# A transformer step on one core: modulation rows spaced between written matmuls, and norms' spreads nine matmuls behind their sums

## The chip, the cores and the metric

The kernel runs on one core of a Trainium2 chip. The metric is the device time of one execution in microseconds (us), the median of the runs. The engines are TensorE (PE, matmuls; PEld its weight loads), VectorE (DVE), ScalarE (ACT), GpSimd (POOL) and SyncE (SP, which issues the loads); each works through its instructions in its own order, and semaphores between engines hold an instruction back until its inputs are there.

## What is computed

One step of a two-layer trunk on 640 tokens (128 context, 512 latent) of width 1024, all in float32. Cut to what matters here:

```
def adaln(cond, w, b):                       # six vectors of 1024 for each layer and each cond
    mod = jax.nn.silu(cond) @ w + b          # w: (1024, 6144)
    return jnp.split(mod[:, None, :], 6, axis=-1)
def modulate(x, g, shift, scale):
    return rms_norm(x, g) * (1 + scale) + shift
def swiglu(h, w_in, w_out):
    gt, up = jnp.split(h @ w_in, 2, axis=-1)
    return (jax.nn.silu(gt) * up) @ w_out
...
for l in range(2):
    sh1, sc1, g1, sh2, sc2, g2 = adaln(c, w_mod[l], b_mod[l])      # and the same for c_ctx
    h = modulate(x, norm1_g[l], sh1, sc1)
    o = ab_mixer(h) if l == 0 else attn(h)   # conv module || bidirectional mLSTM; attention
    x = x + g1 * o
    x = x + g2 * swiglu(modulate(x, norm2_g[l], sh2, sc2), w_ffn_in[l], w_ffn_out[l])
```

`cond` is `c` for latent and `c_ctx` for context tokens, so the modulation is a product of two vectors with a 1024 x 6144 matrix in each layer.

## The kernel before

**Tiling.** The activations lie transposed: 8 blocks of 128 features by 640 tokens, the tokens in two halves `a` of `HF` = 320. Each float32 operand is split into a high and a low part (ScalarE copies the high one, L112 for weights and L483 for activations; L115 and L484 subtract it), and `mm3` (L192) makes a product of three matmuls: L195, L196, L197. A weight tile is loaded into one of two `raw` buffers and split into one of six W buffers.

**Order in the program.** The stages follow one another: `ab_layer` (projections, convolution, mLSTM heads), `out_proj`, FFN 0 (`ffn_in`, then `ffn_out_T`), `attn_layer`, `out_proj`, FFN 1 (`ffn_in`, `ffn_out_rows`). The kernel is written so; a scheduler with a timing model of its own then sets the order of each engine's instructions, and `behind(ins)` tells it that what is issued inside has to stand behind the instructions `ins`. `so_far(engine)` is the last instruction written for an engine. All weight loads (`raw<-...`, `mraw<-in_wmod`) go through SP's queue in one order.

**The modulation.** Work on it is a list of generators in the background. The stages call `tick(us, dt)`, which adds `us` of credit and moves `now`; the generators run while there is credit. One that yields a negative number is not called again until `now` has moved by so much. For the first layer, `mod_T` makes 512 columns of the modulation at a time on TensorE: two groups of four matmuls (`mod_rows`, L254, `p<-mraw,cs`), each of which needs four loads of 256 KB into the ring of six `mraw` buffers; then `rows_T` (L270) transposes the rows on VectorE into a `t` buffer, and `mod_cols` (L261, `p<-t,fsel`) picks the columns with four small matmuls, to which L264 adds the bias. For everything behind out_proj the same is done on VectorE (`mod_blocks`, L225 and L227).

**The norms.** `norm_T` gives `tile(k, a)`, which squares a block (L379) and adds the squares up (L382), and `finish(a)`: the sums over the partitions by TensorE (L409, `p<-one,t`), the root on ScalarE (L412), the reciprocal on VectorE (L413), the spread of it over all partitions by TensorE (L417, `p<-ident,col`), then for each pair of blocks the product (L389), scale and shift (L429 on VectorE, L431 on ScalarE) and the split into `H` (L483, L484). There are two halves; `finish(1)` is put into `pending` and called inside the next stage by `pend`. `L497` adds a projection's result to the residual; L1592 is the silu of an FFN and L1593 its product. At the end of the mLSTM, L1154 transposes a head's output and L1156 and L1157 gate it.

Of the kernel before, what the change touches and what calls it, by code (L numbers as in the profile page):

```python
# [46 lines left out]
class Kern:  # L47
    def __init__(self, tc, I, O):
        self.tc, self.nc, self.I, self.O = tc, tc.nc, I, O
        self.psp, self.hold, self.hold_w, self.in_order = None, (), (), False  # L50
        self.bg, self.credit, self.now, self.lo_pool, self.lo_n, self.pending = [], 0.0, 0.0, (2, 3, 4, 5, 6, 7), 0, []
# [140 lines left out]
    def mm3(self, out, w, x, first, last):  # L192

        t = self.nc.tensor
        t.matmul(out, w[0], x[0], start=first, stop=False)  # L195
        t.matmul(out, w[0], x[1], start=False, stop=False)  # L196
        t.matmul(out, w[1], x[0], start=False, stop=last)  # L197
# [68 lines left out]

    def rows_T(self, ps):

        tr = self.rows_tr = self.tt()[:, :512]
        self.nc.vector.transpose(tr, ps)  # L270
        v = tr.rearrange("p (a q n) -> p a q n", q=4, n=32)
        return lambda q: v[:, :, q, 0:2]

    def mod_T(self, l, which, half, out):

        nc = self.nc
        j = 2 * which + half
        if (l, which) < (0, 5):
            ps = self.p1()
            for g in range(2):  # L280
                yield -3
                self.mfill()
                ks = range(4 * g, 4 * g + 4)
                ws = [self.mready.pop(0) for _ in ks]
                assert [key for key, _ in ws] == [(l, j, k) for k in ks]

                with self.tc.manual_schedule(engines={mybir.EngineType.PE}):
                    for (_, _, k), w in reversed(ws):
                        self.mod_rows(ps, k, w)
                self.mfill()  # L290
                yield 0.1
            yield -4
            parts = self.rows_T(ps)
            yield 0.6
        else:
            box = []
            yield from self.mod_blocks(l, j, box)
            r = self.st()[:, :32]
            for c in range(2):
                tr = self.tt()[:, :512]  # L300
                nc.vector.transpose(tr, box[0][:, c])
                nc.vector.tensor_reduce(r[:, c * 16:(c + 1) * 16], tr.rearrange("p (b i) -> p b i", i=32),
                                        axis=AX.X, op=ALU.add)
            v = r.rearrange("p (c a q) -> p a c q", c=2, q=4)
            parts = lambda q: v[:, :, :, q]
        yield -3
        self.mod_cols(l, which, half, out, parts)
        yield 0.1
# [57 lines left out]
    def norm_T(self, xT, m, H, gi):  # L366
# [17 lines left out]
        def finish(a):  # L384
            sl = slice(a * HF, (a + 1) * HF)
            r = self.rstd_P([sums[a][:, :HF]])
            for i in range(4):
# [45 lines left out]
    def pend(self, n):  # L433

        for _ in range(min(n, len(self.pending))):
            self.pending.pop(0)()

# [4 lines left out]
    def proj_A(self, H, *jobs, bg=()):  # L442
# [3 lines left out]
        for a in range(2):  # L446
# [3 lines left out]
            def mm(i, j, ks):  # L450
                w = jobs[i][0][j]
                if ks[0] == 0:
                    if self.pairs and len(jobs[i][0]) == 2:
                        if j == 0:
                            q = self.p2()
                            outs[i, 0], outs[i, 1] = q[:, 0, :HF], q[:, 1, :HF]
                    else:
                        outs[i, j] = self.p1()[:, :HF]
                for k in ks:
                    self.mm3(outs[i, j], (w[0][:, k * P:(k + 1) * P], w[1][:, k * P:(k + 1) * P]),  # L460
                             (H[:, k, 0, sl], H[:, k, 1, sl]), k == 0, k == KD - 1)

            for i, (ws, evac) in enumerate(jobs):
# [36 lines left out]
    def out_proj(self, H, xT, gate, last, norm, parts=(KD - 2,)):  # L500

        tile, finish = norm
        ws = self.wtake(3)

# [13 lines left out]
        for k0, k1 in zip((0,) + parts, parts):  # L518
            for i, a, ps in first:
                mm(ps, i, a, k0, k1)  # L520
                self.tick(8 / len(parts))
                if k1 == KD - 2:
# [8 lines left out]
        for a in range(2):  # L531
            for i in range(len(first) // 2, KD):
                if a == 0 and i > 2:
                    ws += self.wtake(1)
                ps = self.p1()[:, :HF]
                mm(ps, i, a, 0, KD)
                self.add_T(xT, i, a, ps, gate)
                tile(i, a)
                self.tick(5)
                if a == 1:  # L540
                    self.wdone(1)
                    if i == 3 + 0:
                        self.flush()
                        finish(0)
        self.pending.append(lambda: finish(1))
# [613 lines left out]
    def ab_layer(self, H, mods):  # L1159
# [132 lines left out]
        next(hd[1])  # L1292
        self.tick(5)
        next(hd[2])
# [6 lines left out]
        self.wcap = 2  # L1301
        o_in()
        next(hd[2])
# [40 lines left out]
    def attn_layer(self, H, mods):  # L1344
# [38 lines left out]
        for t in range(NT):  # L1383
            ps = self.p1()
            self.proj_B(ps, H, t, ws, 0, 512, 2, 512, 0, 4)
            self.pend(1)
            self.proj_B(ps, H, t, ws, 0, 512, 2, 512, 4)
            if t == 0:
# [228 lines left out]
    def ffn_out_T(self, fs, gs, xT, gate, norm=None):  # L1617

        ws = self.wtake(len(fs))
        for a in range(2):  # L1620
            for k in range(KD):
                ps = self.p1()[:, :HF]
                ks = slice(k * P, (k + 1) * P)
                for i, (g, w) in enumerate(zip(gs, ws)):
                    self.mm3(ps, (w[0][:, ks], w[1][:, ks]),
                             (g[:, a * HF:(a + 1) * HF], g[:, TOK + a * HF:TOK + (a + 1) * HF]),
                             i == 0, i == len(fs) - 1)
                self.add_T(xT, k, a, ps, gate)
                if norm:
                    norm[0](k, a)  # L1630
                    if (k, a) == (1, 1):
                        norm[1](0)
        if norm:
# [245 lines left out]
```

## Time and profile before

| | |
|---|---|
| median of 3 runs | 1563.33 us (1562.85 to 1564.67) |
| profiled execution | 1561.09 us, its span 1559.3 us |
| mean granted TensorE clock | 0.988 |
| TensorE busy | 1517.9 us (97%) |
| VectorE, ScalarE, GpSimd busy | 911.3, 580.9, 540.6 us |
| read from memory | 157.53 MB, 105 GB/s over the span |

Times of the trace count from the span's start. A row of the timeline gives start, duration, engine, line, operation, output and inputs, partitions and elements, the count of merged instructions, and in brackets the idle time of the engine just before it and what ended it. A matmul's duration includes its way through the array: they overlap, and the distance between two starts is what one costs. A row of waits gives who waited for whom: us in total, how often, the longest. A row of windows gives start and end, length, then the busy time of PE, PEld, DVE, ACT and POOL with counts, the granted clock, the share of the DMA engines and GB/s. A row of SP's queue gives the issue of the first load and the time up to the last.

### The profile page before, as it was taken

The numbers are of one execution on the slowest core, as the hardware profiler recorded it, in microseconds if no ns is written. First come the engines' busy times: TensorE is split into PE (matmuls) and PEld (weight loads), VectorE is DVE, ScalarE is ACT, GpSimd is POOL, SyncE is SP. The second block draws the span as 40 slices with busy tenths as digits, with TensorE's granted clock in tenths as the row PEclk, the third lists the DMA queues.
The fourth block names the chain that finished last, engine by engine and source line by source line (L and its number), as shares of the span: only waits on it lengthen the run. The fifth ranks groups of instructions, "written<-read, shape, count | busy, mean of one in ns | idle before, by whom it ended". The sixth has DMA issues, their size and how long they took to land.

```text
span 1559.3 us, 24243 instructions
## 1 busy us (share of the span) xinstructions
PE 1517.9 (97%) x9722; PEld 1411.1 (90%) x9722; DVE 911.3 (58%) x1514; ACT 580.9 (37%) x1151; POOL 540.6 (35%) x366
## 2 busy tenths in 40 slices
PE   8999999799999999999999999999999999999998
PEld 7889888679999999999998877799998998999996
DVE  5799523448983785637668588835663423333335
ACT  5756557225312221212126438624431221312123
POOL 3387312122222221222132455422225523334341
PEclk9999999899999999999999999999999999999999
DMA  9322122622542343314243220032321221312211
GB/s 368 126 100 93 61 89 90 229 98 95 200 152 83 121 155 103 130 60 154 91 166 118 82 81 28 22 128 82 109 95 55 81 82 55 108 55 93 70 68 68
DMA packets 63850, 165.36 MB, mean 106 GB/s; under 512 B 6904, under 2 KB 14112, under 8 KB 63738
## 3 DMA queue, kind: packets, MB, share of 16 engines
q1 hardware_dynamic: 63194, 163.16, 30.4%
q8 instruction: 76, 1.25, 0.3%
q10 hardware_dynamic: 544, 0.66, 0.1%
q14 instruction: 36, 0.29, 0.1%
HBM read 157.53 MB, written 6.26 MB: 105 GB/s over the span
## 4 chain that ended last, share of the span: by engine, by line
PE 82%; DVE 9%; ACT 3%; DMA 3%; issue 2%; POOL 1%; SPq 0%; ACTq 0%; DVEq 0%; POOLq 0%
PE p L195 25%; PE p L197 24%; PE p L196 24%; DVE cy L863 3%; PE p L254 1%; DMA mraw<-in_wmod 1%; PE p L1489 1%; DMA h<-in_xT 1%; DVE acc L227 1%; POOL t L872 1%; DVE H L484 1%; PE p L1509 1%; DVE h L497 1%; DMA h<-in_wmod 0%; ACT w L112 0%
## 5 line engine op out<-in xcount | busy, mean ns | idle before, releaser
L195 PE MATMUL p<-H,w 128*128 128x320 f32 (+1 forms) x1968 | 609.3, 311 | 4.0 <-DVE modT L264 1.6
L197 PE MATMUL p<-H,w 128*128 128x320 f32 (+1 forms) x1968 | 609.2, 310 | 0.0
L196 PE MATMUL p<-H,w 128*128 128x320 f32 (+1 forms) x1968 | 607.4, 309 | 0.6 <-DVE H L484 0.6
L115 POOL TENSOR_TENSOR w<-raw,w 128x1024 fp32r<-128x1024 f32 x124 | 310.4, 2508 | 751.1 <-ACT w L112 723.7
L195 PEld LDWEIGHTS p<-H,w 128*128 128x128 f32 x1968 | 371.0, 189 | 9.5 <-issue 1.7
L196 PEld LDWEIGHTS p<-H,w 128*128 128x128 f32 x1968 | 371.2, 189 | 1.6 <-DVE H L484 0.9
L197 PEld LDWEIGHTS p<-H,w 128*128 128x128 f32 x1968 | 370.8, 188 | 1.3 <-issue 1.1
L112 ACT ACTIVATE w<-raw 128x1024 fp32r<-128x1024 f32 x180 | 189.0, 1057 | 385.9 <-PE p L197 274.5
L227 DVE SCALAR_TENSOR_TENSOR acc<-mraw,cs,acc 128x512 f32<-128x512 f32 x196 | 176.8, 947 | 0.0
L1593 DVE TENSOR_TENSOR t<-t,p 128x320 f32<-128x320 f32 x88 | 42.6, 484 | 180.4 <-ACT t L1592 178.4
L1592 ACT ACTIVATE t<-p 128x320 f32<-128x320 f32 x88 | 38.3, 436 | 229.5 <-PE p L197 229.4
L115 DVE TENSOR_TENSOR w<-raw,w 128x1024 fp32r<-128x1024 f32 x56 | 78.3, 1399 | 64.2 <-ACT w L112 64.1
L497 DVE SCALAR_TENSOR_TENSOR h<-p,modT,h 128x128 f32<-128x128 f32 (+2 forms) x189 | 74.9, 431 | 60.2 <-PE p L197 59.9
L195 PE MATMUL p<-h,w 128*128 128x320 f32 x352 | 109.1, 310 | 0.0
L196 PE MATMUL p<-h,w 128*128 128x320 f32 x352 | 108.5, 308 | 0.0
L197 PE MATMUL p<-h,w 128*128 128x320 f32 x352 | 108.5, 308 | 0.0
L484 DVE TENSOR_TENSOR h<-t,h 128x320 fp32r<-128x320 f32 x88 | 85.9, 977 | 32.4 <-ACT h L483 32.4
L490 DVE TENSOR_TENSOR t<-p,h 128x512 f32<-128x512 f32 (+1 forms) x61 | 41.4, 681 | 83.7 <-PE p L197 83.6
L195 PE MATMUL p<-w,h 128*128 128x512 f32 (+1 forms) x224 | 87.9, 392 | 0.0
L196 PE MATMUL p<-w,h 128*128 128x512 f32 (+1 forms) x224 | 87.8, 392 | 0.0
L491 POOL TENSOR_TENSOR h<-h,t 128x512 f32<-128x512 f32 x50 | 69.5, 1394 | 51.9 <-DVE t L490 51.8
L197 PE MATMUL p<-w,h 128*128 128x512 f32 (+1 forms) x224 | 87.4, 390 | 0.0
(332 smaller groups left out, 2156.5 us busy)
## 6 DMA issues: line engine op xcount, KB each, us to landing
raw<-in_wfi SPq DMA_DIRECT2D x88, 512.0 KB
mraw<-in_wmod SPq DMA_DIRECT2D x160, 256.0 KB
raw<-in_wfo SPq DMA_DIRECT2D x44, 512.0 KB
raw<-in_wab SPq DMA_DIRECT2D x16, 512.0 KB
raw<-in_wc SPq DMA_DIRECT2D x12, 512.0 KB
h<-in_xT SPq DMA_DIRECT2D x14, 320.0 KB
h<-in_wmod SPq DMA_DIRECT2D x8, 512.0 KB
raw<-in_woab SPq DMA_DIRECT2D x8, 512.0 KB
```

What stands on the lines that cost most here:

```text
L112: self.hi_last = self.nc.scalar.activation(hi, r, AF.Copy).ins,
L115: e.tensor_tensor(lo, r, hi.bitcast(F32), ALU.subtract)
L195: t.matmul(out, w[0], x[0], start=first, stop=False)
L196: t.matmul(out, w[0], x[1], start=False, stop=False)
L197: t.matmul(out, w[1], x[0], start=False, stop=last)
L227: nc.vector.scalar_tensor_tensor(acc[:, c], w, s, bias if k == 0 else acc[:, c], ALU.mult, ALU.add)
L484: j = self.nc.vector.tensor_tensor(lo, src, hi.bitcast(F32), ALU.subtract)
L490: nc.vector.tensor_tensor(tmp, ps, gate, ALU.mult)
L491: (e or nc.gpsimd).tensor_tensor(x, x, tmp, ALU.add)
L497: self.nc.vector.scalar_tensor_tensor(x, ps[:, b - a * HF:e - a * HF], gate[:, k, c:c + 1], x, ALU.mult, ALU.add)
L863: nc.vector.scalar_tensor_tensor(y, u[:, i:i + CONV_N], w(i), y, ALU.mult, ALU.add)
L1593: nc.vector.tensor_tensor(s[:, sl], s[:, sl], pu, ALU.mult)
```

## The change

Three things are edited.

1. **The groups' pace.** A generator now waits six units of `now` between a set's two groups and none ahead of the first; in out_proj each piece gives credit by its number of blocks, and two `tick` calls in `ab_layer` give other numbers. Each group is set `behind` the last matmul written so far (`tied`, up to out_proj).
2. **The transposed rows** go into the first of the group's own `mraw` buffers instead of a `t` buffer.
3. **The norms.** `finish` becomes a generator that stops between the root and the spread. `pend` starts it (sums and root); `pend_rest`, called by the following stage after its first nine matmuls (after blocks 4 and 5 in attention's first stage), issues the rest behind them, and `mm3` sets the next product's first matmul behind the spread (`then`).

```diff
@@ mm3
-        t.matmul(out, w[0], x[0], start=first, stop=False)
+        with self.behind(self.then):
+            t.matmul(out, w[0], x[0], start=first, stop=False)
@@ rows_T
-    def rows_T(self, ps):
+    def rows_T(self, ps, tr=None):
 
-        tr = self.rows_tr = self.tt()[:, :512]
+        tr = self.rows_tr = self.tt()[:, :512] if tr is None else tr
@@ mod_T
             for g in range(2):
-                yield -3
+                if g:
+                    yield -6
...
-                with self.tc.manual_schedule(engines={mybir.EngineType.PE}):
+                with self.behind(self.so_far(mybir.EngineType.PE) if self.tied else ()), \
+                        self.tc.manual_schedule(engines={mybir.EngineType.PE}):
...
-            parts = self.rows_T(ps)
+            parts = self.rows_T(ps, ws[0][1])
@@ finish
-            r = self.rstd_P([sums[a][:, :HF]])
+            root = self.rstd_steps([sums[a][:, :HF]])
+            next(root)
+            yield
+            r = next(root)
@@ pend
-            self.pending.pop(0)()
+            g = self.pending.pop(0)()
+            if g:
+                next(g)
+                self.begun.append(g)
+
+    def pend_rest(self):
+
+        while self.begun:
+            with self.behind(self.so_far(mybir.EngineType.PE)):
+                for _ in self.begun.pop(0):
+                    pass
+            self.then = self.so_far(mybir.EngineType.PE)
@@ proj_A, in its loop over k (ffn_out_T the same with i == 2)
+                    if k == 2:
+                        self.pend_rest()
@@ out_proj
+        self.tied = False
...
-                self.tick(8 / len(parts))
+                self.tick(8 if len(parts) == 1 else (k1 - k0) * 0.45)
...
-                mm(ps, i, a, 0, KD)
+                mm(ps, i, a, 0, 3)
+                self.pend_rest()
+                mm(ps, i, a, 3, KD)
...
                     if i == 3 + 0:
+                        self.pending.append(lambda: finish(0))
+                        self.pend(1)
                         self.flush()
-                        finish(0)
@@ ab_layer
-        self.tick(5)
+        self.tick(5, 2)
...
-        o_in()
+        o_in(6, 14)
@@ attn_layer
             self.pend(1)
-            self.proj_B(ps, H, t, ws, 0, 512, 2, 512, 4)
+            self.proj_B(ps, H, t, ws, 0, 512, 2, 512, 4, 6)
+            self.pend_rest()
+            self.proj_B(ps, H, t, ws, 0, 512, 2, 512, 6)
@@ ffn_out_T
-                        norm[1](0)
+                        self.pending.append(lambda: norm[1](0))
+                        self.pend(1)
```

The edits shift the lines: L195 to L197 become L196 to L198, L254 and L261 become L255 and L262, L382 becomes L385, L389 L395, L409 L415, L412 L418, L413 L419, L417 L423, L429 L435, L484 L503, L497 L516, L1593 L1618.

What the built programs show at four places follows. In the first, TensorE's order in out_proj of the first layer before (`mraw,cs` the groups, `t,fsel` the columns, `ident,h` the transposes of the mLSTM's output):

```order
L261 MATMUL p_3141<-t,fsel 32x8 x4
L254 MATMUL p_3147<-mraw,cs 32x512 x8
L261 MATMUL p_3210<-t,fsel 32x8 x4
L254 MATMUL p_3216<-mraw,cs 32x512 x4
L1154 MATMUL p_3266<-ident,h 128x128
L1154 MATMUL p_3265<-ident,h 128x128 x4
L254 MATMUL p_3216<-mraw,cs 32x512 x4
L1154 MATMUL p_3277<-ident,h 128x128
```

And around one of its groups now:

```order
L197 MATMUL p_3411<-H,w 128x320
L198 MATMUL p_3411<-H,w 128x320
L255 MATMUL p_3365<-mraw,cs 32x512 x4
L196 MATMUL p_3455<-H,w 128x320
L197 MATMUL p_3455<-H,w 128x320
L198 MATMUL p_3455<-H,w 128x320
```

A group that stood beside other groups now stands between written products of out_proj; the next group's or columns' matmuls are 45 or more matmuls away, and the whole layer's twelve groups are placed like this, eight of them ahead of out_proj.

The second is SP's queue of loads around out_proj, before (`woab` out_proj's weights, `wfi` those of FFN 0):

```order
L99 DMA raw<-in_woab 128x1024 x3
L99 DMA mraw<-in_wmod 128x512 x24
L1326 DMA out_new_n<-s 8x128
L99 DMA raw<-in_wfi 128x1024 x8
L99 DMA mraw<-in_wmod 128x512 x4
```

And now:

```order
L99 DMA raw<-in_woab 128x1024 x3
L99 DMA mraw<-in_wmod 128x512 x8
L1349 DMA out_new_n<-s 8x128
L99 DMA mraw<-in_wmod 128x512 x3
L99 DMA raw<-in_wfi 128x1024
L99 DMA mraw<-in_wmod 128x512 x2
L99 DMA raw<-in_wfi 128x1024 x2
L99 DMA mraw<-in_wmod 128x512 x4
```

The run of 24 loads of the modulation is now in pieces of two to eight, earlier in the program or between the loads of FFN 0's weights.

The third is VectorE at FFN 0's start, the second half of its norm, before:

```order
L382 TENSOR_TENSOR t<-t 128x320 x2
L497 SCALAR_TENSOR_TENSOR h<-p_3707,modT,h 128x320
L382 TENSOR_TENSOR t<-t 128x320
L413 RECIPROCAL col<-col 128x3
L389 TENSOR_TENSOR t<-h,p_3810 128x640 x4
L1593 TENSOR_TENSOR t<-t,p_3778 128x320
L429 TENSOR_SCALAR t<-t,modT 128x320 x4
L484 TENSOR_TENSOR h<-t,h 128x320
L484 TENSOR_TENSOR H<-t,H 128x2x320 x3
```

And now:

```order
L385 TENSOR_TENSOR t<-t 128x320 x2
L516 SCALAR_TENSOR_TENSOR h<-p_3701,modT,h 128x320
L385 TENSOR_TENSOR t<-t 128x320
L419 RECIPROCAL col<-col 128x3
L1618 TENSOR_TENSOR t<-t,p_3772 128x320
L503 TENSOR_TENSOR h<-t,h 128x320
L395 TENSOR_TENSOR t<-h,p_3818 128x640 x4
L435 TENSOR_SCALAR t<-t,modT 128x320 x4
L503 TENSOR_TENSOR H<-t,H 128x2x320 x2
```

The silu's product (L1618) and its split (L503, `h<-t,h`) now stand ahead of the norm's four products (L395) instead of behind them.

The fourth is TensorE at attention's start, before:

```order
L195 MATMUL p_8358<-w,H 128x512
L196 MATMUL p_8358<-w,H 128x512
L197 MATMUL p_8358<-w,H 128x512
L409 MATMUL p_8371<-one_87,t 128x1 x3
L417 MATMUL p_8378<-ident,col 128x128 x2
L417 MATMUL p_8378<-ident,col 128x64
L195 MATMUL p_8432<-w,H 128x512
```

And now:

```order
L196 MATMUL p_8352<-w,H 128x512
L197 MATMUL p_8352<-w,H 128x512
L198 MATMUL p_8352<-w,H 128x512
L415 MATMUL p_8365<-one_87,t 128x1 x3
L423 MATMUL p_8378<-ident,col 128x128 x2
L423 MATMUL p_8378<-ident,col 128x64
L196 MATMUL p_8352<-w,H 128x512
```

The sums and the spread still stand next to each other; both now come two blocks (six matmuls) ahead of the end of the first 24 matmuls, where they stood behind all 24.

More of the change, by code (lines that the diff above doesn't have):

```diff
@@ L49, in __init__ @@
         self.tc, self.nc, self.I, self.O = tc, tc.nc, I, O
-        self.psp, self.hold, self.hold_w, self.in_order = None, (), (), False
+        self.psp, self.hold, self.hold_w, self.in_order, self.begun, self.then, self.tied = None, (), (), False, [], (), True
         self.bg, self.credit, self.now, self.lo_pool, self.lo_n, self.pending = [], 0.0, 0.0, (2, 3, 4, 5, 6, 7), 0, []
@@ L1627, in ffn_out_T @@
                              i == 0, i == len(fs) - 1)
+                    if i == 2:
+                        self.pend_rest()
                 self.add_T(xT, k, a, ps, gate)
```

## The prediction

> **What bounds the kernel now.** I read the page first, for which engine carries the time, then the list of waits of TensorE, then the timeline around each wait, and last the stages' windows, for the clock.
>
> ```profile
> PE 1517.9 (97%) x9722; PEld 1411.1 (90%) x9722; DVE 911.3 (58%) x1514; ACT 580.9 (37%) x1151; POOL 540.6 (35%) x366
> PE 82%; DVE 9%; ACT 3%; DMA 3%; issue 2%; POOL 1%; SPq 0%; ACTq 0%; DVEq 0%; POOLq 0%
> ...
> PE p L254 <- DMA mraw<-in_wmod: 9.9, 5, 3.5
> PE p L417 <- DVE col L413: 5.3, 5, 2.3
> PE p L1067 <- ACT s L1109: 1.0, 1, 1.0
> PE p L905 <- DVE t L270: 0.8, 1, 0.8
> ```
>
> TensorE is busy for 1517.9 of the 1559.3 us, and the change removes no matmul. So only two things can be won: the idle time of TensorE (1559.3 − 1517.9 = 41.4 us, part of it at the ends) and time that it spends at half clock. The two largest single waits are those the change aims at: the rows of the modulation (L254) waiting for their loads, 9.9 us in 5 waits, and the spread of a norm's root (L417) waiting for the reciprocal, 5.3 us in 5. Most of the first lies in the output projection (out_proj) of the first layer, so I opened that stretch:
>
> ```profile
> 301.12 1.07 PE L254 MATMUL p<-mraw,cs 128*32 128x512 f32 x8 [1.47 <-DMA mraw<-in_wmod]
> 305.68 1.94 PE L254 MATMUL p<-mraw,cs 128*32 128x512 f32 x8 [3.50 <-DMA mraw<-in_wmod]
> 308.53 0.30 PE L261 MATMUL p<-t,fsel 128*32 128x8 f32 x8 [0.92 <-DVE t L270]
> 311.06 1.94 PE L254 MATMUL p<-mraw,cs 128*32 128x512 f32 x8 [2.24 <-DMA mraw<-in_wmod]
> 313.85 1.11 PE L1154 MATMUL p<-ident,h 128*128 128x128 f32 x4 [0.45 <-DVE h L1156]
> 316.40 1.94 PE L254 MATMUL p<-mraw,cs 128*32 128x512 f32 x8 [1.44 <-DMA mraw<-in_wmod]
> 322.67 0.41 PE L195 MATMUL p<-H,w 128*128 128x320 f32 x1 [0.74 <-DVE h L1157]
> ...
> 302.50:319.60 17.10, 8.89 (x42) 3.07 (x43) 3.76 (x7) 0.74 (x1) 0.00 (x0) 0.50 0.55 187
> 290.84 29.85 SPq L99 DMA_DIRECT2D mraw<-in_wmod  x24
> ```
>
> The number in brackets is the idle time before a row. Together they make 10.76 us. The queue row says why: 24 loads in one run, 29.85 / 24 = 1.24 us each, so a group of four needs 5.0 us, while its matmuls last 1.07. The window row adds the second cost: over 17.10 us the granted clock is 0.50, and a group takes 1.94 instead of 1.07 us.
>
> **The change, part by part.**
>
> **Groups apart, in out_proj.** Before, six groups stand nearly back to back there. After, the twelve groups of the whole layer are spread; four are left in out_proj, with 45 or more matmuls between neighbours. A matmul of 320 columns starts every 0.15 us (rows of 373.46 and 373.61, below), so 45 of them last 6.6 us, which is the smallest distance between two groups; four loads take 5.0. The loads' waits (8.65 us) and the wait for the rows' transpose (0.92) go. What stays is the end of the mLSTM: 0.45 and 0.74 are waits for its outputs, and its ten transposes now stand in one piece, with no group between them to cover VectorE; I add 0.8 and keep 2.0 us idle. That gives 10.76 − 2.0 = 8.8. The half clock: 8.89 us of work at 1.94/1.07 of its length is 8.89 × (1 − 1.07/1.94) = 4.0 too long; with 2.0 us of waits left I keep one half chance of a short period at half clock (0.9) and count 3.1. **Sum +11.9**; ends: 5 (loads at half the rate, below) and 14.
>
> **The other eight groups, in the layer's projections.** Their waits are in these rows:
>
> ```profile
> 240.70 1.06 PE L254 MATMUL p<-mraw,cs 128*32 128x512 f32 x8 [1.23 <-DMA mraw<-in_wmod]
> 150.00:290.00 140.00, 135.43 (x937) 121.29 (x939) 66.73 (x157) 83.61 (x226) 42.23 (x29) 0.96 0.31 99
> ```
>
> The 1.23 and the 0.8 before L905 go with the groups that caused them. Against that, ScalarE's order now mixes sigmoid and silu, two table loads more (1.28 each, row of 372.29 below); ScalarE is busy for 83.61 of 140 us, so I let a fifth of them reach TensorE. The loads now enter SP's queue earlier, and four of them stand between the first and the second weight tile of the V projection; four loads are 5.0 us, and the group that frees their buffers now stands 72 matmuls (10.6 us) ahead of that projection, so I cost it at nothing, covered by those matmuls; without that cover up to 5.0. The transposed rows now lie in one of the six load buffers until L261 has read them, so one buffer comes free later: five are enough for a group of four. **Sum +1.5**; ends −5.0 (all of the V tiles' delay) and +4 (also the 1.0 of L1067).
>
> **FFN 0: spread nine matmuls behind the sums.**
>
> ```profile
> 349.44 0.85 PE L417 MATMUL p<-ident,col 128*128 128x128 f32 x6 [1.04 <-DVE col L413]
> 371.25 0.72 PE L409 MATMUL p<-one,t 128*128 128x1 f32 x6
> 372.54 0.88 PE L417 MATMUL p<-ident,col 128*128 128x128 f32 x6 [0.56 <-DVE col L413]
> 373.46 0.31 PE L196 MATMUL p<-H,w 128*128 128x320 f32 x1
> 373.61 0.31 PE L197 MATMUL p<-H,w 128*128 128x320 f32 x1
> ...
> 372.29 1.28 ACT L1592 ACT_TABLE_LOAD   x1
> 373.58 0.44 ACT L1592 ACTIVATE t<-p 128x320 f32<-128x320 f32 x1
> 373.45 3.01 DVE L389 TENSOR_TENSOR t<-h,p 128x640 f32<-128x640 f32 x4 [0.97 <-PE p L417]
> 376.38 0.48 DVE L1593 TENSOR_TENSOR t<-t,p 128x320 f32<-128x320 f32 x1
> 378.21 0.48 DVE L484 TENSOR_TENSOR h<-t,h 128x320 fp32r<-128x320 f32 x1
> 378.61 2.29 DVE L484 TENSOR_TENSOR H<-t,H 128x640 fp32r<-128x640 f32 x3
> 481.21 0.39 PE L195 MATMUL p<-H,w 128*128 128x320 f32 x1 [1.59 <-DVE modT L264]
> ```
>
> Nine matmuls last 9 × 0.147 = 1.32 us, more than the 0.56 and the 1.04 that were waited: +1.60. But VectorE's order changes with it. Call T the end of the sums (371.97). Before, L389 begins at T + 1.5 and the first quarter of the second half of H is ready at T + 7.45 (378.61 + 0.8); 48 matmuls and the spread stand before its first reader, at T + 8.3, so 0.9 is to spare. After, the silu product (L1593) and its split (L484 h) stand ahead of L389. They wait for the root (0.3), the table load (1.28), silu (0.44), the product (0.48), the copy on ScalarE (about 0.45) and the split (0.48): L389 begins at T + 3.65, and H is ready 5.2 later (the same work less those two), at T + 8.8. The reader comes at T + 7.8. New wait 1.05, a little more for the later quarters: −1.15. TensorE then comes to the modulation's wait at 481.21 earlier than VectorE does: −0.7; and the sums may wait 0.2. **Sum −0.5**; ends −3.5 and +1.6.
>
> **Attention's start.**
>
> ```profile
> 826.49 0.85 PE L417 MATMUL p<-ident,col 128*128 128x128 f32 x6 [0.82 <-DVE col L413]
> 841.71 0.40 PE L197 MATMUL p<-w,H 128*128 128x512 f32 x1
> 841.95 0.39 PE L195 MATMUL p<-w,H 128*128 128x512 f32 x1
> 844.16 0.83 PE L409 MATMUL p<-one,t 128*128 128x1 f32 x6 [0.18 <-DVE t L382]
> 845.55 0.88 PE L417 MATMUL p<-ident,col 128*128 128x128 f32 x6 [0.56 <-DVE col L413]
> ...
> 827.38:844.10 16.72, 16.37 (x96) 14.61 (x95) 16.51 (x28) 10.39 (x22) 3.60 (x2) 1.00 0.38 139
> ```
>
> Here the change works against itself. The first spread loses its 0.82 us of waiting, but stands 1.32 behind the sums, 0.5 later than before, and it starts a chain on VectorE that has no gap: 16.51 of 16.72 us busy until the squares are summed. So the second half's sums can begin at 844.16 + 0.5 = 844.66. TensorE would reach them at 841.95 − 0.82 = 841.13, because they now stand six matmuls of 0.23 us earlier; and the spread follows them at once, as before. It waits 3.5, then 0.56, and then has the six matmuls to do (1.4): it stands at 848.14 where it stood at 846.24, **−1.9**. A wait of 3.5 us should also halve the clock, for which the nearest row is this one:
>
> ```profile
> 1063.89 1.51 PE L417 MATMUL p<-ident,col 128*128 128x128 f32 x6 [2.30 <-DVE col L413]
> 1063.90:1067.10 3.20, 3.20 (x13) 3.20 (x14) 1.66 (x3) 0.80 (x2) 0.48 (x1) 0.50 0.65 230
> 1063.59 0.16 DVE L413 RECIPROCAL col<-col 128x3 f32<-128x3 f32 x1
> 1098.49 0.42 PE L196 MATMUL p<-H,w 128*128 128x320 f32 x1 [0.62 <-DVE H L484]
> ```
>
> Idle for 2.30 us was enough there for 3.20 us at clock 0.50, which is 1.6 us of work lost; I take **−1.6** at attention's start. Ends for both: −5 and +0.8.
>
> **FFN 1.** The 2.30 shrinks by the nine matmuls to 2.30 − 1.32 = 0.98, since the reciprocal is itself late (1063.59, 2.0 after the sums): +1.3. With 0.98 idle the 3.20 us at half clock should go (+1.6), as none followed the 1.04 at 349.44. The second spread now stands nine instead of 23 matmuls behind its sums, so H comes earlier and the 0.62 goes. **Sum +3.5**; ends +1 and +4.
>
> [...]
>
> **Together** 11.9 + 1.5 − 0.5 − 1.9 − 1.6 + 3.5 = 12.9 us. The profiled execution took 1561.09 us (span 1559.3 and 1.8 around it) and would take 1548.2. It stands 2.2 below the median of the runs, 1563.33; from the median the sum gives 1550.4.
>
> **The rivals.**
>
> *The clock stays low.* Waits of 2.0 us in out_proj and 0.98 in FFN 1 are shorter than 2.30, but the window 150:290 shows a mean clock of 0.96 with no TensorE wait above 1.23 in it, so 2.30 is no threshold. If both places keep a period at half clock, 0.9 + 0.7 in out_proj's remainder and 1.6 in FFN 1 are lost: gain 9.7, 1553.6. Chance 15%.
>
> *The loads are still late.* They now share the queues with weight tiles, as they did not in the run of 24. At twice the time for each, 2.5 us, a group needs 10 where the shortest distances are 6.6 and 8.7: some 4.7 us of waits and half of the 4.0 at low clock remain, gain about 6.2, 1557.1. Against it: the 24 loads moved 6 MB in 29.85 us, a rate the mixed queue has no reason to halve. Chance 10%. If the layer's loads come as late as before, the change does not do what it says: only the norms' parts remain, −0.5 of them net, and the time is within 0.2% of 1563 (that bound, 3.1 us, is about what a measurement of this kernel can tell from no change). Chance 7%.
>
> *More is won.* The low clock in 150:290 is worth 2 × 0.04 × 140 = 11 us at half speed, 5.6 us of work. If evenly placed groups keep TensorE fed there, half to all of it comes back: 1545 to 1548. Nothing shows that the groups caused it. Chance 13%.
>
> *Slower.* Each transposed group must have been through VectorE (L270) before L261 stands on TensorE, now written straight ahead of the next group. If VectorE, which works through its orders in sequence, is late, all of TensorE's work stands behind L261. The rows show 0.8 and 0.92 for two of these waits. Six of them must last 12.9 / 6 = 2.2 us each to eat the gain, and 2.7 to be measured as slower; at 3 us the time is 1568. Against it: 40 to 70 matmuls, 6 us or more, lie between a group's last rows and its L261, and VectorE is busy for 67 of 140 us. Chance 6%.
>
> **How the numbers follow.** The forecast has the other 49%, its own range is 1547 to 1553.5, and its time, 1550.4, is the prediction. The range 1542 to 1559 leaves out the last two cases with no gain and the far ends of the others, some 18%. Faster: 49 + 15 + 10 + 13 = 87, less 2 for loads worse than doubled: 85%. Same 8%, slower 7%.
>
> **What would show it.** Right: no wait of L254 for its loads above 0.5 us and clock 1.00 in out_proj; the spread's waits gone at FFN 0, but 1 us before the first matmul on the second half of H; sums at attention's start waiting 3 to 4 us, with a period at 0.50 behind; at FFN 1 a wait near 1 and clock 1.00. Wrong: waits of L261 for VectorE, of TensorE for V's weight tiles near 60 to 75 us, or a junction wait at FFN 0 of 3 us.

## Result: 1545.6 us, 1.1% faster

| | before | changed |
|---|---|---|
| median, runs made together | 1563.77 us (4 runs) | 1545.63 us (4 runs, 1544.78 to 1550.6) |
| ratio to before | | 0.9891, 95% interval 0.9869 to 0.9912 |
| profiled execution | 1561.09 us | 1544.78 us |
| span | 1559.3 us | 1542.8 us |
| TensorE busy | 1517.9 us | 1511.4 us |
| mean granted clock | 0.988 | 0.994 |

The profiled executions differ by 16.3 us, the medians by 18.1; the sum of the prediction, 12.9, is held against the first. These are the page's first row and the head of TensorE's waits after the change:

```profile
PE 1511.4 (98%) x9722; PEld 1407.5 (91%) x9722; DVE 912.9 (59%) x1514; ACT 581.6 (38%) x1153; POOL 540.9 (35%) x366
...
PE p L415 <- DVE t L385: 3.6, 1, 3.6
PE p L196 <- ACT t L861: 1.9, 2, 1.7
PE p L679 <- POOL ident masks.py:199: 1.6, 1, 1.6
PE p L415 <- DVE t L654: 1.6, 1, 1.6
PE p L196 <- DVE modT L265: 1.6, 1, 1.6
PE p L423 <- DVE col L419: 1.3, 2, 0.8
PE p L197 <- POOL w L115: 1.3, 1, 1.3
```

The busy time alone fell by 6.5 us although every matmul is still there: that is time at half clock that is gone (a mean granted clock of 0.994 instead of 0.988). The other 10 us of the span are idle time. The loads of the groups, 9.9 us before, have left the head of the list; a wait for the sums of a norm (L415) now leads it.

**Where it came from.** The matmuls of `mm3` are numbered from 0 in order of time in both traces, and the starts of the n-th are compared. The cuts at 1400, 4600 and 5500 lie shortly ahead of the first sums of a norm, so that each norm falls into one row. The table gives by how much the changed kernel is ahead, and what each stretch adds:

| up to | n | before, us | changed, us | ahead by | stretch |
|---|---|---|---|---|---|
| within the V projection | 300 | 82.57 | 87.82 | -5.3 | -5.3 |
| rest of the first layer, with out_proj's first matmuls | 1200 | 292.62 | 292.11 | +0.5 | +5.8 |
| most of out_proj, to FFN 0's first sums | 1400 | 345.33 | 329.06 | +16.3 | +15.8 |
| FFN 0 and its norm, to attention's first sums | 4600 | 823.56 | 805.87 | +17.7 | +1.4 |
| attention and its norm, to FFN 1's first sums | 5500 | 1057.96 | 1045.20 | +12.8 | -4.9 |
| FFN 1's norm and its first matmuls | 6100 | 1158.61 | 1142.12 | +16.5 | +3.7 |

Two of the groups (2 x 1.06 us) moved from behind the 1200th matmul to ahead of it, so out_proj itself won 13.7 and the layer 2.6. In out_proj the rows that answer to the seven waits of before are these, and the window's clock:

```profile
296.94 1.06 PE L255 MATMUL p<-mraw,cs 128*32 128x512 f32 x8 [0.87 <-DMA mraw<-in_wmod]
301.05 0.66 PE L1177 MATMUL p<-ident,h 128*128 128x128 f32 x4 [0.51 <-DVE h L1180]
310.30 1.07 PE L255 MATMUL p<-mraw,cs 128*32 128x512 f32 x8
319.39 1.06 PE L255 MATMUL p<-mraw,cs 128*32 128x512 f32 x8
...
290.00:340.00 50.00, 48.61 (x345) 44.07 (x342) 27.11 (x59) 18.70 (x42) 14.15 (x9) 1.00 0.42 143
150.00:290.00 140.00, 137.99 (x1000) 122.77 (x998) 69.59 (x159) 88.05 (x234) 43.64 (x30) 1.00 0.36 119
```

Of 10.76 us of waits 1.38 are left, the clock is 1.00 where it was 0.50 for 17.1 us, and a group takes 1.06 instead of 1.94. The last row is the layer ahead of it: its clock went from 0.96 to 1.00, which the forecast had left to a rival.

Where the change lost, the profile of before had shown it at one place and not at the other. Attention's start:

```profile
827.27 0.83 PE L415 MATMUL p<-one,t 128*128 128x1 f32 x6 [3.58 <-DVE t L385]
828.66 1.54 PE L423 MATMUL p<-ident,col 128*128 128x128 f32 x6 [0.56 <-DVE col L419]
...
828.10:834.90 6.80, 6.24 (x19) 5.17 (x19) 4.73 (x11) 2.91 (x11) 0.00 (x0) 0.50 0.13 45
```

The sums wait 3.58 us, the spread 0.56, and 6.80 us at clock 0.50 follow. And the V projection, here TensorE's rows and SP's queue:

```profile
53.19 0.39 PE L196 MATMUL p<-H,w 128*128 128x322 f32 x1 [1.05 <-ACT h L437]
59.72 0.42 PE L196 MATMUL p<-H,w 128*128 128x322 f32 x1 [1.71 <-ACT t L861]
78.92 0.50 PE L197 MATMUL p<-w,H 128*128 128x512 f32 x1 [1.27 <-POOL w L115]
...
48.02 0.33 SPq L99 DMA_DIRECT2D raw<-in_wv  x1
58.02 1.75 SPq L99 DMA_DIRECT2D mraw<-in_wmod  x4
59.82 11.99 SPq L99 DMA_DIRECT2D raw<-in_wv  x3
...
60.10:63.50 3.40, 3.40 (x15) 3.40 (x14) 3.07 (x6) 1.98 (x6) 0.00 (x0) 0.50 0.90 273
```

Four loads of the modulation are sent only at 58.02, when the group at 56.94 has read their buffers, and three of the four weight tiles of V stand behind them in the same queue; the split (L115) of one of them is then late at 78.92. But the weight tiles are the smaller part. At the 200th matmul, ahead of V, 4.9 us are already lost: the two waits for ScalarE (1.05 and 1.71, where before had 0.42), 1.7 of the 3.4 us at half clock, and the group's own 1.06, which before came behind that point.

### The profile page after: what moved, and what is told of

Same layout as the page of the kernel before. It is cut to its first block, busy times and chain, and to the rows that moved or that the text cites. A ratio compares the mean times of both kernels' runs of the same rounds, so it can differ in the third digit from the quotient of the medians.

```text
span 1542.8 us, 24258 instructions
## 1 busy us (share of the span) xinstructions
PE 1511.4 (98%) x9722; PEld 1407.5 (91%) x9722; DVE 912.9 (59%) x1514; ACT 581.6 (38%) x1153; POOL 540.9 (35%) x366
## 4 chain that ended last, share of the span: by engine, by line
PE 83%; DVE 6%; ACT 4%; DMA 3%; POOL 2%; issue 2%; SPq 0%; ACTq 0%; DVEq 0%; POOLq 0%
PE p L196 25%; PE p L198 25%; PE p L197 25%; POOL t L895 2%; PE p L255 1%; DMA raw<-in_wab 1%; ACT w L112 1%; PE p L1514 1%; DVE cy L886 1%; POOL w L115 1%; PE p L1534 1%; DVE H L503 1%; DMA h<-in_wmod 0%; PE p L1536 0%; PE p L1535 0%
## 5 line engine op out<-in xcount | busy, mean ns | idle before, releaser
L196 PE MATMUL p<-H,w 128*128 128x320 f32 (+1 forms) x1968 | 609.5, 311 | 5.1 <-ACT t L861 1.9
L198 PE MATMUL p<-H,w 128*128 128x320 f32 (+1 forms) x1968 | 608.8, 310 | 0.0
L197 PE MATMUL p<-H,w 128*128 128x320 f32 (+1 forms) x1968 | 606.9, 309 | 0.0
L115 POOL TENSOR_TENSOR w<-raw,w 128x1024 fp32r<-128x1024 f32 x124 | 312.0, 2521 | 738.6 <-ACT w L112 723.1
L196 PEld LDWEIGHTS p<-H,w 128*128 128x128 f32 x1968 | 370.0, 188 | 15.2 <-issue 3.4
L198 PEld LDWEIGHTS p<-H,w 128*128 128x128 f32 x1968 | 370.1, 188 | 1.3 <-issue 1.1
L197 PEld LDWEIGHTS p<-H,w 128*128 128x128 f32 x1968 | 370.5, 188 | 0.7 <-issue 0.2
L1618 DVE TENSOR_TENSOR t<-t,p 128x320 f32<-128x320 f32 x88 | 42.5, 483 | 181.1 <-ACT t L1617 180.7
L115 DVE TENSOR_TENSOR w<-raw,w 128x1024 fp32r<-128x1024 f32 x56 | 79.3, 1416 | 67.4 <-ACT w L112 67.3
L196 PE MATMUL p<-h,w 128*128 128x320 f32 x352 | 109.1, 310 | 0.0
L197 PE MATMUL p<-h,w 128*128 128x320 f32 x352 | 108.5, 308 | 0.0
L198 PE MATMUL p<-h,w 128*128 128x320 f32 x352 | 108.5, 308 | 0.0
L516 DVE SCALAR_TENSOR_TENSOR h<-p,modT,h 128x128 f32<-128x128 f32 (+2 forms) x189 | 74.9, 430 | 55.5 <-PE p L198 55.4
L503 DVE TENSOR_TENSOR h<-t,h 128x320 fp32r<-128x320 f32 x88 | 85.9, 976 | 35.7 <-ACT h L502 35.7
L196 PE MATMUL p<-w,h 128*128 128x512 f32 (+1 forms) x224 | 87.9, 392 | 0.0
L197 PE MATMUL p<-w,h 128*128 128x512 f32 (+1 forms) x224 | 87.8, 392 | 0.0
L198 PE MATMUL p<-w,h 128*128 128x512 f32 (+1 forms) x224 | 87.4, 390 | 0.0
```

Source lines behind the costliest of these rows:

```text
L115: e.tensor_tensor(lo, r, hi.bitcast(F32), ALU.subtract)
L503: j = self.nc.vector.tensor_tensor(lo, src, hi.bitcast(F32), ALU.subtract)
L516: self.nc.vector.scalar_tensor_tensor(x, ps[:, b - a * HF:e - a * HF], gate[:, k, c:c + 1], x, ALU.mult, ALU.add)
L1618: nc.vector.tensor_tensor(s[:, sl], s[:, sl], pu, ALU.mult)
```

## Experiments

All times are medians; each ratio is to the kernel before, run in turn with it on the same chip.

**1. The groups alone.** The norms as before, run through at once at their old places.

```diff
-            if g:
-                next(g)
-                self.begun.append(g)
+            for _ in g or ():
+                pass
...
@@ out_proj
+                        self.flush()
                         self.pending.append(lambda: finish(0))
                         self.pend(1)
-                        self.flush()
```

> The changed kernel with the norms as they were: root and spread at once, at the old places; the groups' pace, ties and transposed rows as changed. Theory A (the gain comes from the loads of the groups, which no longer arrive in one run, and from the clock that the waits had halved): nearly all of it is here, since the norms' part sums to about zero over its four places (FFN 0 +1.6, attention -5.0, FFN 1 +3.7): 16 us below the kernel before, profiled time near 1545, out_proj at clock 1.00; at attention's start a wait of the spread of 0.8 and of 0.6 again and no period at half clock behind it, at FFN 1 the 2.3 and the half clock again. Rival B (the norms' part carries the gain, since it takes waits away at five places): 1556 or more.

Measured: 1544.24 us (1542.64 to 1550.07), ratio 0.9883 (0.9861 to 0.9905), profiled 1542.64. Out_proj is at clock 1.00. The groups alone carry the whole gain: theory A holds, B falls.

**2. The norms alone.** The kernel before with root and spread apart.

> The kernel before with the norms' part alone; pace, ties and transposed rows as before. Theory A: no gain to speak of, within 1 us of the kernel before, the waits in out_proj unchanged (10 to 11 us), at attention's start sums that wait 3.6 us and half clock for about 6.8 us behind. Rival B: 5 us or more faster. Rival C (the two parts help each other, because a norm's place depends on the groups around it): e1 and e2 together fall short of the whole gain of 16.3 by 3 us or more.

Measured: 1563.29 us (10 runs), ratio 0.9999 (0.9989 to 1.001). The waits of out_proj are there unchanged, and so is the new wait at attention's start:

```profile
PE p L255 <- DMA mraw<-in_wmod: 9.8, 5, 3.4
PE p L414 <- DVE t L384: 3.6, 1, 3.6
...
844.90:851.80 6.90, 5.06 (x18) 4.50 (x19) 3.23 (x7) 1.94 (x5) 0.00 (x0) 0.51 0.39 130
```

The norms' part is worth nothing as a whole. The two gains, 19.4 and 0.4 us by the medians, leave nothing for rival C.

**3. The credit in out_proj as before**, all else as changed:

```diff
-                self.tick(8 if len(parts) == 1 else (k1 - k0) * 0.45)
+                self.tick(8 / len(parts))
```

> The changed kernel with out_proj's old credit for the background, all else as changed: the last four groups then stand 38 and 23 matmuls apart and the last two back to back, behind a run of 12 loads, where the changed kernel has 39 to 110 matmuls between them. Theory A (a group waits when the matmuls since the group before it last less than its four loads, 5 us): no wait at the first, 23 matmuls last 3.4 us, so 1 to 2 us of waits there, then about 4 to 5 us at the last group (four loads less what is loaded ahead), and a period at half clock of 3.4 us or more: 5 to 9 us slower than the changed kernel. Rival (the ties and the layer's pace before out_proj made the gain, and the ring of six hides the loads): within 1.5 us of the changed kernel.

Measured: 1553.92 us (1551.73 to 1557.5), ratio 0.9944 (0.9929 to 0.9959), 8.3 us slower than the changed kernel by the medians.

```profile
304.65 0.25 PE L262 MATMUL p<-mraw,fsel 128*32 128x8 f32 x8 [0.58 <-DVE mraw L271]
309.91 1.79 PE L255 MATMUL p<-mraw,cs 128*32 128x512 f32 x8 [4.07 <-DMA mraw<-in_wmod]
312.60 0.30 PE L262 MATMUL p<-mraw,fsel 128*32 128x8 f32 x8 [0.90 <-DVE mraw L271]
...
300.52 12.92 SPq L99 DMA_DIRECT2D mraw<-in_wmod  x12
...
310.10:320.40 10.30, 8.77 (x43) 6.49 (x36) 4.82 (x10) 1.48 (x2) 0.00 (x0) 0.50 0.38 124
```

One pair of groups back to back behind a run of 12 loads is enough for a wait of 4.07 us, two waits for the transpose (0.58 and 0.90) and 10.3 us at half clock. The 1 to 2 us expected at the group 23 matmuls behind its neighbour did not come; tiles loaded ahead may have covered it, which no row here shows. From the 1200th to the 1400th matmul this kernel takes 44.65 us, the changed one 36.96 and the one before 52.71, so one pair of groups gives back half of what out_proj had won. Theory A holds: the distance of a group to the one before it makes the gain.

**4. Without the ties.**

```diff
-                with self.behind(self.so_far(mybir.EngineType.PE) if self.tied else ()), \
+                with self.behind(()), \
```

> The changed kernel without the ties of the groups: the pace alone. The built order then has the first six groups as three pairs, 17 to 24 matmuls apart, and the last six where the changed kernel has them, four of them in out_proj. Theory A (out_proj's gain comes from groups far enough apart for their loads, 45 matmuls or more): out_proj as in the changed kernel, and waits for loads of 1 to 2 us at the second group of each pair: 2 to 5 us slower than the changed kernel, or less where VectorE's chain at 164 us takes it back. Rival (the tie makes the gain): 1555 or more.

Measured: 1542.6 us (1537.65 to 1543.87), ratio 0.9858 (0.9838 to 0.9878). Out_proj is as in the changed kernel (clock 1.00 in 290:340). The pairs in the layer wait 0.52 and 0.59 us for loads, less than expected, the V projection loses less (its weights' waits are gone), and the 2 to 5 us by which the kernel was to be slower did not come. So the ties make no gain; the interval overlaps that of the changed kernel, so they are not shown to cost anything either.

**5. The first group back** behind V's weights, to its old place:

```diff
                 if g:
                     yield -6
+                elif j == 4:
+                    yield -3
```

> The changed kernel with one line added, a wait of three units ahead of the first set of rows, which puts its first group back behind the V projection's four weight loads in the queue and to its old place on TensorE; all other groups stay. Theory A: the 5.2 us that the changed kernel loses by the V projection (waits of 1.05, 1.71 and 1.27 between 53 and 79 us and 3.4 us at half clock) come from this group and its four loads standing between the V weights: 4 to 5 us faster than the changed kernel, 1540. Rival: they come from the other order of ScalarE's work in the stretch, which stays: under 1.5 us faster.

Measured: 1544.29 us (1541.86 to 1546.98), ratio 0.9877 (0.986 to 0.9893). At the 300th matmul it is 6.6 us ahead of the changed kernel, at the 800th 1.1. Of this 1.2 stand already at the 100th, far ahead of the group: the clock from 19.2 to 22.4 us is 0.50 in the changed kernel and 1.00 here. So the group's place wins 5.4 us up to the 300th matmul, and all of it is gone by the 800th. The row in which most of it went, and what VectorE does at that time:

```profile
163.58 0.39 PE L196 MATMUL p<-H,w 128*128 128x320 f32 x1 [2.84 <-DVE t L1116]
...
148.03 15.01 DVE L888 SCALAR_TENSOR_TENSOR cy<-t,vecs,cy 128x655 f32<-128x655 f32 x16
162.95 0.48 DVE L1116 TENSOR_TENSOR t<-p,t 128x128 f32<-128x128 f32 x2
...
164.60:168.00 3.40, 3.40 (x15) 3.40 (x14) 3.35 (x5) 1.74 (x7) 1.43 (x1) 0.50 0.49 154
```

VectorE has 16 taps of the convolution (L888) ahead of the mLSTM's product (L1116). TensorE, which came earlier, waits 2.84 us for it and loses 1.7 in the clock. Theory A was half right: the 5 us up to V come with the first group's place, but winning them is worth nothing here, because VectorE's convolution takes them back 80 us later. The edit moves the group and its four loads together, so it doesn't tell the queue's part from the group's.

**6. Attention's second norm behind all 24 matmuls again**, the first spread still nine behind.

```diff
-            self.proj_B(ps, H, t, ws, 0, 512, 2, 512, 0, 4)
-            self.pend(1)
-            self.proj_B(ps, H, t, ws, 0, 512, 2, 512, 4, 6)
-            self.pend_rest()
-            self.proj_B(ps, H, t, ws, 0, 512, 2, 512, 6)
+            self.proj_B(ps, H, t, ws, 0, 512, 2, 512)
+            with self.behind(self.so_far(mybir.EngineType.PE)):
+                self.pend(1)
+            self.pend_rest()
```

> The changed kernel with attention's second half of the norm back behind all 24 matmuls of the first tile, sums and spread together, as before the change. Theory A (VectorE's chain without a gap sets when the sums can begin, whatever stands on TensorE): the sums wait 3.58 - 1.40 = 2.2 instead of 3.6 us, the spread 0.56 again, 1.4 us gained and, if the period at half clock goes or halves, 1.7 to 3.4 more: 1.4 to 4.8 us faster than the changed kernel. Rival (the six matmuls earlier cost nothing, since the wait moves with them): 0.3 us or less.

Measured: 1544.65 us (1543.82 to 1544.89), ratio 0.9878 (0.9863 to 0.9893). From the 4600th to the 4800th matmul it takes 49.43 us, the changed kernel 50.82.

```profile
826.90 0.50 PE L197 MATMUL p<-w,H 128*128 128x512 f32 x1 [1.76 <-DVE w L115]
828.50 1.38 PE L415 MATMUL p<-one,t 128*128 128x1 f32 x6 [0.17 <-DVE t L385]
830.44 1.54 PE L423 MATMUL p<-ident,col 128*128 128x128 f32 x6 [0.56 <-DVE col L419]
...
828.60:835.40 6.80, 6.24 (x21) 5.38 (x22) 3.56 (x8) 3.59 (x12) 0.00 (x0) 0.50 0.24 90
```

Theory A holds at its low end: 1.4 us are won at the junction. Ahead of the sums TensorE waits 1.93 us (2.2 expected), most of it a few matmuls earlier than thought, for a weight split (L115) that stands in the same chain on VectorE; and half clock followed for as long as before, so nothing came back of the clock. In the whole time the 1.4 us don't show: the intervals of the two kernels overlap.

**7. Attention's first spread back behind its sums**, the second norm as changed. `True` has `pend` run the norm through at once.

```diff
                         self.pending.append(lambda: norm[1](0))
-                        self.pend(1)
+                        self.pend(1, True)
```

> The changed kernel with only attention's first spread (at the end of FFN 0) back to its old place straight behind its sums; the second keeps its place behind 18 matmuls. It tells the two causes at attention's start apart. Theory A (VectorE's chain sets the sums, and it starts 0.5 us later for the nine matmuls): the spread waits 0.8 again, the sums wait 3.58 - 0.82 - 0.5 = 2.3 us instead of 3.6, in all 0.5 us faster, and up to 3.4 more if 2.3 us no longer halve the clock. Rival (the delay of the first spread is the whole loss): the sums wait under 1 us and nearly all of the 4.9 us come back.

Measured: 1545.13 us (1544.21 to 1547.2), ratio 0.9882 (0.9866 to 0.9897).

```profile
810.61 0.85 PE L423 MATMUL p<-ident,col 128*128 128x128 f32 x6 [0.82 <-DVE col L419]
828.28 1.44 PE L415 MATMUL p<-one,t 128*128 128x1 f32 x6 [2.06 <-DVE t L385]
830.29 1.01 PE L423 MATMUL p<-ident,col 128*128 128x128 f32 x3 [0.56 <-DVE col L419]
...
828.20:835.00 6.80, 6.15 (x20) 5.39 (x21) 3.33 (x7) 1.38 (x5) 0.00 (x0) 0.50 0.43 155
```

The wait at the sums is 2.06, near theory A's 2.3, and the stretch from the 4600th to the 4800th matmul takes 50.00 us, 0.8 less than in the changed kernel (0.5 expected). Half clock is as long as in the changed kernel: 6.80 us stand at the waits of 2.06 and 0.56 us, 2 us apart.

**8. Both of attention's norms as before, those of the FFNs as changed.**

```diff
@@ attn_layer
-            self.pend(1)
-            self.proj_B(ps, H, t, ws, 0, 512, 2, 512, 4, 6)
-            self.pend_rest()
-            self.proj_B(ps, H, t, ws, 0, 512, 2, 512, 6)
+            self.pend(1, True)
+            self.proj_B(ps, H, t, ws, 0, 512, 2, 512, 4)
@@ ffn_out_T
-                        self.pend(1)
+                        self.pend(1, True)
```

> The changed kernel with attention's two norms (the first spread, at the end of FFN 0, and the second, in attention's first tile) whole and at their old places; the norms of FFN 0 and FFN 1 keep their nine matmuls. Theory A (each place adds up by itself): attention's start gets back what it lost, 4.9 us, as in the run with the groups alone; the FFNs keep the 1.3 and 2.0 us that they have over that run: profiled 1544.8 - 4.9 = 1540, some 3 us under the groups alone, and no half clock at attention. Rival (the whole norms' part is worth nothing, it only shifts waits): 1543 to 1544, like the groups alone.

Measured: 1540.84 us (1540.3 to 1547.12), ratio 0.9862 (0.9841 to 0.9883). From the 4600th to the 4800th matmul it takes 45.74 us, 5.1 less than the changed kernel and as much as the kernel before (45.82), and the clock there is 1.00:

```profile
806.00:840.00 34.00, 32.22 (x189) 28.65 (x188) 29.57 (x58) 22.32 (x47) 4.94 (x4) 1.00 0.37 134
```

So each of the two moves at attention's start, taken back alone, returns a part of the waits (1.4 and 0.8 us in 6 and 7), and only taking back both returns the clock as well: each alone leaves two periods at half clock. The profiled execution (1543.36) had three such periods in the first layer; the median fits theory A, though its interval overlaps those of the changed kernel and of experiment 1.

**9. The same with the first group back.**

> The same with the first group back behind the V projection's weights as well. Theory A (the convolution's chain on VectorE takes back at 164 us what the V projection wins, as the run with the first group back alone showed: 6.3 won, 4.6 given back there): within 1 us of the run without this line, 1539 to 1540.5. Rival (the 4.6 were a period at half clock that need not come again): 1536 or less.

Measured: 1540.2 us (1538.73 to 1541.89), ratio 0.9849 (0.9833 to 0.9865). The interval lies just below that of the changed kernel, so this version beats it as well as the kernel before; it isn't told apart from experiment 8, nor quite from experiment 1, the groups alone.

**10. That one without the ties.**

> The fastest kernel so far (FFN norms only, first group back) without the ties. Theory A (the ties do nothing that the scheduler's own order does not do as well; what is left to win are periods at half clock, whose places change from kernel to kernel): 1537 to 1541, no difference beyond the interval. Rival (the ties cost 3 us, as the untied kernel's lower median suggests): 1535 to 1538.

Measured: 1542.79 us (1537.21 to 1545.98), ratio 0.9871 (0.9853 to 0.989). No difference beyond the intervals, as theory A said, though the median lies above the 1537 to 1541 expected. Its own runs are spread over 8.8 us.

## Why the prediction came out as it did

**Right, with its mechanism: out_proj.** Expected +11.9, measured 13.7. The waits fell from 10.76 to 1.38 us, not to 2.0, and the term of 0.9 for one more short period at half clock was not needed. Experiments 1 and 3 show the cause: the gain comes with the groups, and half of it goes with the distance of the last two.

What is left of the waits is not what the sum had named: 0.87 of it is a group waiting for its loads, where none above 0.5 was to come. That group stands 38 matmuls (5.6 us) behind its neighbour, not 45 or more. And the 1.24 us are not the time of one load. Before, SP's queue and TensorE took turns:

```profile
302.16 1.75 SPq L99 DMA_DIRECT2D mraw<-in_wmod  x4
```

The four loads are sent within 1.75 us, as soon as the group at 301.12 has read the buffers, and the next group starts at 305.68, 3.5 us after the first of them was sent. So 5.0 us is the round of one group, its own matmuls and the way of the next loads. It came out as a usable size for the distance, but the distance is counted from the end of the group before: in the changed kernel the loads around the group at 296.94 leave from 290.68 on, behind the group at 289.27, and loads in out_proj took 2.4 to 6.1 us to land.

**Right: attention's wait.** 3.5 us were expected at the sums, 3.58 came. What was sized wrong is the clock behind it, 6.80 us at 0.50 instead of 3.20, so 3.4 lost instead of 1.6; the stage lost 4.9 instead of 3.5.

**Right in sum: FFN 1**, +3.7 against +3.5, with a wait of 0.77 where 0.98 was worked out, and clock 1.00:

```profile
1051.04 0.88 PE L423 MATMUL p<-ident,col 128*128 128x128 f32 x6 [0.77 <-DVE col L419]
1051.00:1058.00 7.00, 6.96 (x49) 6.96 (x50) 6.04 (x8) 4.99 (x10) 3.00 (x2) 1.00 0.32 118
```

But the step that the wait alone makes its clock term of 1.6 doesn't hold. In experiment 1 the same spread waits the same 2.30 us, and no half clock follows:

```profile
1046.92 0.85 PE L423 MATMUL p<-ident,col 128*128 128x128 f32 x6 [2.30 <-DVE col L419]
1044.00:1054.00 10.00, 7.70 (x57) 7.65 (x56) 8.96 (x18) 7.02 (x15) 1.94 (x2) 1.00 0.36 107
```

**Wrong: FFN 0's new wait.** The step "the reader comes at T + 7.8" failed. VectorE and H are as worked out; here the sums, the first quarter of H's low part, and TensorE's readers:

```profile
353.82 0.77 PE L415 MATMUL p<-one,t 128*128 128x1 f32 x6
362.46 1.56 DVE L503 TENSOR_TENSOR H<-t,H 128x640 fp32r<-128x640 f32 x2
362.48 1.00 PE L196 MATMUL p<-H,w 128*128 128x320 f32 x5
363.32 0.30 PE L197 MATMUL p<-H,w 128*128 128x320 f32 x1
```

And TensorE's readers before:

```profile
380.34 0.90 PE L195 MATMUL p<-H,w 128*128 128x320 f32 x5
381.08 0.31 PE L196 MATMUL p<-H,w 128*128 128x320 f32 x1
```

T is 354.59; the low part is ready at 362.46 + 0.8 = 363.26, T + 8.7 (8.8 was expected). But at T + 7.9 there stand five matmuls in a row (L196) that read only the high part, which ScalarE writes. The first reader of the low part (L197) comes at 363.32, T + 8.7, and they cover all but some 0.35 us of the wait: the five start 0.40 us behind the matmul before them instead of 0.15, and take 0.84 us where the five of before took 0.74. The order that the sum had worked out was VectorE's; the answer stood in TensorE's, and in the trace of before already, where the five start at T + 8.4 and the reader is at 381.08, T + 9.1, not 8.3. The modulation's wait did not grow either: it is 1.59 us before and after. So FFN 0 won 1.4 instead of losing 0.5.

**Wrong in both directions: the first layer**, 2.6 against 1.5. The delay of V's weight tiles was costed at nothing, as covered by 72 matmuls. V's second tile is not sent before the group's buffers are free, and one tile was waited for 1.27 us. The larger part of the 5.3 us lost there has no term in the sum, which gave ScalarE only a fifth of two table loads: by the first group's new place TensorE waits 1.05 and 1.71 us for ScalarE, and half clock follows. Why ScalarE is late there is not shown. The rest won 7.9: the waits, and three periods at half clock (a mean of 0.96 in 150:290) that became none. This was a rival, at 13%, with the note that nothing showed the groups to be the cause. The runs speak for it: the mean clock in 150:290 is 0.96 and 0.95 in the two kernels with the old pace (before and experiment 2) and 0.98 to 1.00 in the ten with the new one. How many periods are left varies from one of these traces to the next.

Together the errors are +1.8 (out_proj), -1.4 (attention), +0.2 (FFN 1), +1.9 (FFN 0) and +1.1 (first layer), which is 3.6; the ledger by matmuls and the profiled times differ by 0.2. The forecast of 1550.4 was 4.8 us too high: the time lies outside the forecast's own 1547 to 1553.5, inside the wider range, and where the rival of more gain had it. That it came this close is in part luck, since the first layer's 5.3 lost and 7.9 won were both left out of the sum and cancel for the most part.

## What to carry to other kernels

A background task that needs loads is placed by the time of the work between its pieces, against the time from a freed buffer to the landed load. Here, in the changed kernel, 38 matmuls (5.6 us) between two groups in out_proj left a wait of 0.87 us for the loads, and the others there, with 54 or more, had none. The run of such pieces at the end of a stage was paid twice here, by 10.76 us of waits and by 17.1 us at half clock. Before a root or a spread is moved to hide its latency, look at what its result starts: where it starts a chain on an engine without a gap, what is lost at the head is waited for at the end (attention's first products on VectorE, 810.06 in the changed kernel and 827.38 before, begin 2.88 instead of 2.51 us behind the start of their sums, and the next sums wait 3.58 us, against 2.06 in experiment 7, where the spread is back at its old place and waits 0.82 itself), and in SP's queue a load that waits for its buffer holds up what stands behind it (four loads sent only at 58.02, three of V's weight tiles from 59.82 on, a wait of 1.27 us at 78.92). A wait that is found early in a program may be one that a later chain would have asked for anyway (experiment 5: 5.4 us won by the 300th matmul, gone by the 800th), so measure it at the next place where the engines meet. And compare two traces stretch by stretch: 1.4 us won at one place can be lost from view in the whole time (experiment 6).

## What the runs showed of the hardware

Periods at half clock wander. In the rows above they last 3.40 us (from 60.10 in the changed kernel, from 164.60 in experiment 5) or 6.80 (attention's start), and in out_proj 10.30 (experiment 3) and 17.10 (before). They come with 2.06 + 0.56 us of idle time in experiment 7, do not come with 2.30 us in experiment 1 and did come with the same 2.30 us before the change. Some stand where TensorE hardly waited: before, the clock is 0.50 from 186.6 to 189.8 us, and no wait above 0.4 us stands in the 7 us ahead. Executions of one and the same kernel differ by them: experiment 1 ran at mean clocks of 0.998, 0.998, 0.995 and 0.993 in 1542.64, 1543.58, 1544.9 and 1550.07 us. From 0.998 to 0.993 is 0.005 x 1541 = 7.7 us, and 7.4 were measured; the run at 0.995 is 2.3 us behind the first where the same working gives 4.6, so this holds only roughly. What sets a period off is not shown: the same wait of 2.30 us halved the clock once and once not, and in experiment 7 the longest wait at the 6.80 us at half clock was 2.06. In this kernel, then, differences of some 3 us between variants are within what the clock alone makes, and the profiled execution of a variant is one draw.
